# Pools per k tile at a seam, an interleaved last tile pair, a partial sum through DRAM and earlier conditioning products in a hybrid SSD trunk

## The chip, the cores and the metric

The kernel runs on one NeuronCore of a Trainium2 chip. The metric is the device time of one execution in microseconds; a lower one is better. Five engines work side by side, each from its own queue in order: TensorE (PE) with its weight loads (PEld), VectorE (DVE), ScalarE (ACT), GpSimd (POOL) and SyncE (SP). DMA transfers are issued from the queues of SP, ACT and POOL, and sixteen DMA engines carry them.

## The reference

One residual layer over a sequence of 1024 positions with 1024 channels. What matters here:

```python
u = rms_norm(x, ln1) * (1 + scale1) + shift1        # scale, shift, gate: silu(c) @ w_ada + b_ada
gl, cb, cc, cx, z, xbc, dt = split(u @ w_in)        # 2048, 3 x 1024, 2048, 4096, 32 columns
p_conv = (cb * causal_conv3(cc * cx)) @ w_conv_out
xbc = silu(causal_conv4(xbc) + b); xs, bs, cs = split(xbc)
y = ssd_scan(xs * dt, -exp(a_log) * dt, bs, cs) + d_skip * xs     # 8 groups, 32 heads, state 128
y = group_rms_norm(y * silu(z)) * ssm_norm_w
p_ssm = y @ w_ssm_out                                # 2048 -> 1024
x = x + gate1 * ((sigmoid(gl_c) * p_conv + sigmoid(gl_s) * p_ssm) @ w_o)
x = x + gate2 * (square(relu(u2 @ w_up)) @ w_down)   # u2 from x as u, then a final rms_norm
```

The conditioning vectors (six times 1024 numbers) come from a matrix-vector product with w_ada.

## The kernel before

Everything is held transposed: channels on the 128 partitions, the 1024 positions along the free dimension in two halves of 512 columns (H). A float32 product is made of three matmuls in a rounded format: each operand is split into a high part (a cast, on ACT) and a low part (source minus high, on DVE), and high x high, high x low and low x high are added in PSUM. `proj` (L125) does this for one output tile: eight k tiles, two halves, 48 matmuls; `load_w` (L90) loads and splits a weight tile, and `load_w_acc` (L99) gets the low part by an accumulating DMA from POOL instead. `strassen_pair` (L145) makes two output tiles with seven products of half the size, 84 matmuls in place of 96, and needs more sums on DVE. It is used for the last eight gate tiles, for z and for the short convolution; its operands T1 to T4 ("tops") are sums of u's quarters.

The kernel runs through these stages, in the order of the program:

1. norm and modulation of x into the operands uh and ul (L245 to L520), with the first eight gate tiles (gl) as they become ready. uh and ul are 32 tiles of 2 KB per partition, all in one pool `u` on the right side of SBUF;
2. the tops (L526 to L540), in place in the memory of x, four pools xk0 to xk3 of 8 KB, which are then released. On the same memory follows the small pool `p0d` for the dt projection (L541 to L563), and after it `pe1`, the working pool of the Strassen pairs: s12 and s34 of 4 KB, two each of cu, cq, cy of 2 KB, and one buffer wv of 4.1 KB;
3. Strassen pairs for the remaining gates (f = 8 to 14), for z (eight pairs, one per group) and for the short convolution (twelve pairs). The 32 remaining conditioning products (`gemvs`, L569) lie in this stage, four ahead of each of two gate pairs and three ahead of each z pair: each loads a 512 KB row block of w_ada into wv from POOL's queue, and a DVE pass (L319) multiplies it by c and sums it up into a column of mcol. The buffer wv is single, so a load waits for the product before it;
4. for each of eight groups, four xbc tiles (`proj_group` L719, `xbc_tile` L706: projection, copy of both halves into a padded row raw, two activations from PSUM into cacc, three taps on DVE, silu), and beside the next group's tiles the SSD scan of this one (`ssd_group` L731, chunks of 128 positions);
5. the seam (L844): u is released, and on its memory a ring of eight buffers ys of 8 KB (`yy`) is laid. First they hold the eight split tiles of the short convolution's output (loaded through three buffers ccs), the operands of w_conv_out, beside the last group's scan (L860);
6. the SSD projection in four quarters b of four k tiles each (L874 to L930), every quarter eight output tiles f of 24 matmuls. b = 0 writes its partial result to DRAM (s_d). At b = 1 the memory of the scan is released, slots are laid there (`sl`), the stored sums are loaded into them and added to; b = 2 adds and gates, b = 3 adds and splits the merged result. The scale of groups 4 to 7 (`finish` L806, `rstd` L822), which b = 2 needs, is made within b = 0;
7. w_o, then the MLP with Strassen products, and the final norm.

The order of the instructions in each queue is not that of the program: a planner (`schedule_with_timeline_sim=True`) writes it ahead of time from its own model of durations, taking the earlier instruction of the program first among those that it holds to be ready. Pools with `reuse_waits="tile"` let a tile on released memory start once the memory under that tile is free.

Of the kernel before, what the change touches and what calls it, by code (L numbers as in the profile page):

```python
# [8 lines left out]
F32 = mybir.dt.float32  # L9
F32R = mybir.dt.float32r  # L10
# [6 lines left out]
P = 128  # L17
T = 1024
# [20 lines left out]
def hybrid_trunk(tc, xT, par, hrows, crow, wada1, wadak, wada2, win, wdt, wco, wso, wo, wup, wdt_, wdn, out):  # L39
# [3 lines left out]
    def tt(o, a, b, op, eng=dve):  # L43
        return eng.tensor_tensor(out=o, in0=a, in1=b, op=op)  # L44
# [80 lines left out]
    def proj(w, xh, xl, nk=KT, base=0, halves=(0, 1), width=H):  # L125
        wh, wl = w
        ps = [mm.tile([P, H], F32, name="mm")[:, :width] for _ in halves]
        for k in range(nk):
            c0 = base + k * P
            mm3(ps, wh[:, c0:c0 + P], wl[:, c0:c0 + P], [xh[k][h] for h in halves], [xl[k][h] for h in halves],  # L130
                k == 0, k == nk - 1)
        return ps
# [118 lines left out]
    hb = d0.tile([P, 64], F32, name="hb")[:, 0:32]  # L251
    z2 = d0.tile([P, NC_ * NH], F32, name="z2")

    up = tc.alloc_tile_pool(name="u", bufs=1, side="right")
    uh = [[up.tile([P, H], F32R, name=f"uh{k}{h}") for h in (0, 1)] for k in range(KT)]
    ul = [[up.tile([P, H], F32R, name=f"ul{k}{h}") for h in (0, 1)] for k in range(KT)]

    cbp = tc.alloc_tile_pool(name="cbp", bufs=1)
    glp = tc.alloc_tile_pool(name="glp", bufs=2)
# [58 lines left out]
    def gemv(w_, o):  # L318
        return dve.tensor_tensor_reduce(out=w_, in0=w_, in1=cb, scale=0.5, scalar=prm[:, BADA + o:BADA + o + 1],  # L319
                                        op0=ALU.mult, op1=ALU.add, accum_out=mcol[:, o:o + 1])  # L320
# [208 lines left out]
    for k in range(4):  # L529
        tks.append(tc.alloc_tile_pool(name=f"tk{k}", bufs=1, side="right", reuse_waits="tile"))  # L530
        with tc.issue_after(rdy.ins):
            ts4 = tops_of(xt[k] + xt[k + 4], mcol[:, 4 + k:5 + k], dc1[:, k:k + 1])
        for i, t in enumerate(ts4):
            o = [tks[-1].tile([P, H], F32R, name=f"t{i}{j}") for j in (0, 1)]
            split(*o, t)
            X[f"T{i + 1}"].append(o)
        X["11"].append([uh[k][0], ul[k][0]])
        X["21"].append([uh[k + 4][0], ul[k + 4][0]])
        X["22"].append([uh[k + 4][1], ul[k + 4][1]])
        xk[k].release()  # L540
    p0d = tc.alloc_tile_pool(name="p0d", bufs=1, reuse_waits="tile")  # L541
    wdr = p0d.tile([P, KT, NH], F32, name="wdr")
    sp.dma_start(wdr, wdt)
    wd = p0d.tile([P, KT, 2 * NH], F32R, name="wd")
# [15 lines left out]

    act.copy(z2, ps[:, :C2])

    p0d.release()  # L563
    ps0.release()

    pe1 = tc.alloc_tile_pool(name="pe1", bufs=2, reuse_waits="tile")
    gem = iter(range(32))

    def gemvs(n):  # L569
        for _, i in zip(range(n), gem):  # L570
            w_ = pe1.tile([P, T + 32], F32, name="wv", bufs=1)[:, 0:T]
            pool.dma_start(w_, wada2[i])  # L572
            gemv(w_, 16 + i)

    def as3(a):
        return a.rearrange("p (c h) -> p c h", c=NC_)

# [25 lines left out]
    for f in range(8, 16, 2):  # L603
        ts_ = [glp.tile([P, T], F32, name="glt") for _ in (0, 1)]

        def gl_ev(i, h, src):
            act.activation(ts_[i][:, hs[h]], src, AF.Tanh, scale=0.5)

        if f == 10:
            dt_chain()  # L610
        elif f > 10:
            gemvs(4)
        strassen_pair(pe1, win[f], win[f + 1], X, gl_ev)
        for i in (0, 1):
            act.dma_start(gl_d[f + i], ts_[i])
    for g in range(NG):
        ts_ = [glp.tile([P, T], F32, name="glt") for _ in (0, 1)]

        def z_ev(i, h, src):
            t = ts_[i][:, hs[h]]  # L620
            act.activation(t, src, AF.Tanh, scale=0.5)
            stt(t, t, 1.0, src, ALU.add, ALU.mult)

        gemvs(3)
        strassen_pair(pe1, win[gtile(g) + 4], win[gtile(g) + 5], X, z_ev)
        for i in (0, 1):
            act.dma_start(z_d[2 * g + i], ts_[i])
# [70 lines left out]
    psB = tc.alloc_tile_pool(name="psB", bufs=1, space=PSUM)  # L698
    psC = tc.alloc_tile_pool(name="psC", bufs=1, space=PSUM)

    padded = [p2t.tile([P, T + 3], F32, name=f"raw{i}", bufs=1) for i in (0, 1)]
    for raw in padded:
        pool.memset(raw[:, 0:3], 0.0)
    padded = itertools.cycle(padded)

    def xbc_tile(win_i, ci, dst):  # L706
        ps = proj(load_w_acc(win[win_i]), uh, ul)
        raw = next(padded)
        for h in (0, 1):
            act.copy(raw[:, 3 + H * h:3 + H * h + H], ps[h])  # L710
        a = p2t.tile([P, T], F32, name="cacc")
        for h in (0, 1):
            act.activation(a[:, hs[h]], ps[h], AF.Identity, bias=hb[:, ci:ci + 1], scale=hw[:, 4 * ci + 3:4 * ci + 4])  # L713
        for j in (2, 1, 0):
            stt(a, raw[:, j:j + T], hw[:, 4 * ci + j:4 * ci + j + 1], a, ALU.mult, ALU.add)
        act.activation(dst, a, AF.Tanh)
        stt(dst, dst, 1.0, a, ALU.add, ALU.mult)

    def proj_group(g):  # L719
        pg = p2g[g % 2]  # L720
        xs = pg.tile([P, 2, T], F32, name="xs")
        bf = pg.tile([P, T], F32, name="bf")
        cf = pg.tile([P, T], F32, name="cf")
        b = gtile(g)
        xbc_tile(b + 0, 2 * g, xs[:, 0, :])
        xbc_tile(b + 1, 2 * g + 1, xs[:, 1, :])
        xbc_tile(b + 2, 16 + g, bf)
        xbc_tile(b + 3, 24 + g, cf)
        return xs, bf, cf

    def ssd_group(g, xs, bf, cf, prev):  # L731
# [106 lines left out]
    for g in range(NG - 1):  # L838
# [2 lines left out]
        while prev is None:  # L841
            prev = drive(gen)
        cur = proj_group(g + 1)
    up.release()  # L844

    yy = tc.alloc_tile_pool(name="yy", bufs=8, side="right", reuse_waits="tile")
    yc = []
    for f in range(8):
        ccs = pcf.tile([P, T], F32, name="ccs", bufs=3)
        sp.dma_start(ccs, yc_d[f])  # L850
        y = yy.tile([P, 2, T], F32R, name="ys")
        split(y[:, 0, :], y[:, 1, :], ccs)
        yc.append(y)
    ych, ycl = [[[y[:, i, hs[h]] for h in (0, 1)] for y in yc] for i in (0, 1)]
# [19 lines left out]
    for b in range(4):  # L874
        yh, yl = [], []
        for k in range(4):
            kk = 4 * b + k
            if k % 2 == 0:
                rb_ = p4.tile([P, T], F32, name="rb", bufs=1)
                sp.dma_start(rb_, rst_d[kk // 2].partition_broadcast(P))  # L880
            yr = p4.tile([P, T], F32, name="yr")
            sp.dma_start(yr, y_d[kk])
            stt(yr, yr, prm[:, SNW + kk:SNW + kk + 1], rb_, ALU.mult, ALU.mult)
            ys = yy.tile([P, 2, T], F32R, name="ys")
            split(ys[:, 0, :], ys[:, 1, :], yr)
            yh.append([ys[:, 0, hs[0]], ys[:, 0, hs[1]]])
            yl.append([ys[:, 1, hs[0]], ys[:, 1, hs[1]]])
        if b == 1:
            for p_ in (psC, psB, psA, p2, p2g[1], p2g[0]):
                p_.release()  # L890
            sl = tc.alloc_tile_pool(name="slots", bufs=17, reuse_waits="tile")
            p5 = tc.alloc_tile_pool(name="p5", bufs=2, side="right", reuse_waits="tile")
        for f in range(8):
            if f % 2 == 0:
                w = load_w(wso[b, f // 2])
            if b == 0:
                if f == 2:
                    finish(prev, last_mm[0])
                if f == 5:
                    rstd(1)  # L900
                gt = gp.tile([P, T], F32, name="gt")
                ps = proj(w, yh, yl, nk=4, base=(f % 2) * 512)
                for h in (0, 1):
                    act.copy(gt[:, hs[h]], ps[h])
                act.dma_start(s_d[f], gt)
                continue
            if b > 1:
                gt = gp.tile([P, T], F32, name="gt")
                sp.dma_start(gt, gl_d[8 + f])
            if b == 2:  # L910
                pc = p5.tile([P, T], F32, name="pc")
                sp.dma_start(pc, at_d[f])
            ps = proj(w, yh, yl, nk=4, base=(f % 2) * 512)
            for h in (0, 1):
                if b == 1:
                    at[f][h] = sl.tile([P, H], F32, name=f"s{h}")
                    sp.dma_start(at[f][h], s_d[f, :, hs[h]])
                a = at[f][h]
                if b < 3:
                    tt(a, ps[h], a, ALU.add)  # L920
                if b == 2:
                    stt(a, gt[:, hs[h]], 1.0, a, ALU.add, ALU.mult)
                    tt(a, a, pc[:, hs[h]], ALU.add)
                if b == 3:
                    g_ = gt[:, hs[h]]
                    stt(g_, g_, 1.0, ps[h], ALU.add, ALU.mult)
                    tt(a, a, g_, ALU.add)
                    mh[f][h] = sl.tile([P, H], F32R, name=f"s{h}")
                    ml[f][h] = sl.tile([P, H], F32R, name=f"s{h}")
                    split(mh[f][h], ml[f][h], a)  # L930
    p5.release()
    p4.release()
    gp.release()
    yy.release()
    d0.release()

    xp = tc.alloc_tile_pool(name="x1", bufs=1, side="right", reuse_waits="tile")
# [280 lines left out]
```

## Time and profile before

| | us |
|---|---|
| three runs | 2106.05, 2103.34, 2099.37 |
| their median | 2103.34 |
| the profiled execution | 2105.2 |
| its span, first to last instruction | 2103.4 |
| PE busy in the span | 2072.5 |
| DVE busy | 1473.1 |
| ACT busy | 963.0 |
| POOL busy | 182.6 |
| mean granted clock of PE | 0.992 |

A timeline row gives the start, the duration, the engine and line, the operation, what it writes and reads, and in square brackets how long the engine stood idle before it and what ended that. A row of the waits gives the total in us, the number of times and the longest. A row of the stretches gives the length, then the busy time of PE, weight load, DVE, ACT and POOL with their instructions, then the clock, the DMA engines' busy share and GB/s. Line numbers of helpers (L44 subtract or add, L47 scalar-tensor-tensor, L87 and L94 weight load and cast, L109 split's cast, L154 Strassen matmul, L120 to L123 the matmuls of `proj`, L319 a conditioning product) stand for many callers; the tile's name tells which.

### The profile page before, as it was taken

The numbers are of one execution on the slowest core, as the hardware profiler recorded it, in microseconds if no ns is written. First come the engines' busy times: TensorE is split into PE (matmuls) and PEld (weight loads), VectorE is DVE, ScalarE is ACT, GpSimd is POOL, SyncE is SP. The second block draws the span as 40 slices with busy tenths as digits, with TensorE's granted clock in tenths as the row PEclk, the third lists the DMA queues.
The fourth block names the chain that finished last, engine by engine and source line by source line (L and its number), as shares of the span: only waits on it lengthen the run. The fifth ranks groups of instructions, "written<-read, shape, count | busy, mean of one in ns | idle before, by whom it ended". The sixth has DMA issues, their size and how long they took to land.

```text
span 2103.4 us, 26276 instructions
## 1 busy us (share of the span) xinstructions
PE 2072.5 (99%) x9760; PEld 1698.4 (81%) x9760; DVE 1473.1 (70%) x2310; ACT 963.0 (46%) x1600; POOL 182.6 (9%) x251
## 2 busy tenths in 40 slices
PE   8999999999999999999999999999999999999997
PEld 6878877888888888887878788888888888888887
DVE  8757777776637778877796748745866665658775
ACT  4433232332246768676564531224554454544432
POOL 0000000000000000000000000012000001232213
PEclk8999999999999999999999999999999999999998
DMA  8315645222274555555366676453144347988932
GB/s 327 106 64 187 203 161 194 87 70 74 77 202 111 123 123 136 140 142 137 99 207 219 213 282 198 167 194 118 61 165 165 150 157 268 304 239 254 284 75 81
DMA packets 139666, 345.16 MB, mean 164 GB/s; under 512 B 13153, under 2 KB 48353, under 8 KB 138002
## 3 DMA queue, kind: packets, MB, share of 16 engines
q1 hardware_dynamic: 98258, 200.14, 29.8%
q0 software_dynamic: 27856, 107.49, 18.0%
q10 hardware_dynamic: 13424, 35.85, 4.4%
q8 instruction: 77, 1.26, 0.2%
q14 instruction: 51, 0.42, 0.1%
HBM read 270.88 MB, written 72.55 MB: 163 GB/s over the span
## 4 chain that ended last, share of the span: by engine, by line
PE 87%; issue 8%; DMA 2%; DVE 1%; POOL 1%; ACT 0%; SPq 0%; DVEq 0%; POOLq 0%; ACTq 0%
PE mm L154 25%; PE mm L121 13%; PE mm L123 13%; PE mm L120 13%; PE mm L1111 11%; PE B L761 2%; PE mm L398 2%; PE B L766 2%; PE C L783 1%; PE sx L398 1%; PE st L398 1%; DMA wraw<-in_win 1%; POOL wv L572 1%; PE A L738 1%; DMA x<-in_xT 1%
## 5 line engine op out<-in xcount | busy, mean ns | idle before, releaser
L154 PE MATMUL mm<-t,whi 128*128 128x512 f32 x1104 | 340.9, 391 | 4.6 <-DVE cq L44 4.6
L154 PEld LDWEIGHTS mm<-t,whi 128*128 128x128 f32 x1104 | 207.6, 188 | 49.7 <-DVE cq L44 6.7
L154 PE MATMUL mm<-t,wlo 128*128 128x512 f32 x552 | 214.9, 390 | 0.0
L1111 PE MATMUL mm<-op,whi 128*128 128x512 f32 x672 | 207.0, 389 | 0.0
L121 PE MATMUL mm<-ul,whi 128*128 128x512 f32 x512 | 203.7, 398 | 0.0
L120 PE MATMUL mm<-uh,whi 128*128 128x512 f32 x512 | 203.3, 397 | 0.0
L44 DVE TENSOR_TENSOR wlo<-s,whi 128x1024 fp32r<-128x1024 f32 (+1 forms) x124 | 124.0, 1012 | 63.5 <-ACT whi L159 62.6
L123 PE MATMUL mm<-uh,wlo 128*128 128x512 f32 x512 | 162.3, 395 | 0.0
L44 DVE TENSOR_TENSOR wlo<-wraw,whi 128x1024 fp32r<-128x1024 f32 (+1 forms) x132 | 141.1, 1069 | 22.8 <-ACT whi L94 16.1
L120 PE MATMUL mm<-ys,whi 128*128 128x512 f32 x384 | 148.5, 394 | 3.7 <-ACT ys L109 3.7
L121 PE MATMUL mm<-ys,whi 128*128 128x512 f32 x384 | 148.8, 394 | 0.6 <-DVE ys L44 0.6
L47 DVE SCALAR_TENSOR_TENSOR cacc<-raw,hw,cacc 128x1024 f32<-128x1024 f32 x96 | 122.8, 1279 | 37.7 <-ACT cacc L713 37.0
L1111 PEld LDWEIGHTS mm<-op,whi 128*128 128x128 f32 x672 | 126.1, 188 | 26.2
L154 PE MATMUL mm<-s,whi 128*128 128x512 f32 x448 | 138.0, 389 | 0.7 <-ACT cu L177 0.7
L159 ACT CAST whi<-wraw 128x1024 fp32r<-128x1024 f32 x76 | 63.5, 836 | 157.8 <-PE mm L154 128.5
L1111 PE MATMUL mm<-op,wlo 128*128 128x512 f32 x336 | 130.7, 389 | 0.0
L755 ACT ACTIVATE seg<-acb,acum 128x128 f32<-128x128 f32 x256 | 81.9, 395 | 106.6 <-PE B L761 101.5
L47 DVE SCALAR_TENSOR_TENSOR y<-mm,mcol,y 128x512 f32<-128x512 f32 (+1 forms) x100 | 69.3, 704 | 78.1 <-PE mm L1111 41.3
L94 ACT CAST whi<-wraw 128x1024 fp32r<-128x1024 f32 x52 | 54.6, 1052 | 149.2 <-PE mm L121 127.0
L123 PE MATMUL mm<-ys,wlo 128*128 128x512 f32 x384 | 122.6, 394 | 0.0
L159 ACT CAST whi<-s 128x1024 fp32r<-128x1024 f32 x76 | 79.7, 1050 | 91.4 <-PE mm L154 85.3
L154 PEld LDWEIGHTS mm<-t,wlo 128*128 128x128 f32 x552 | 103.9, 188 | 21.7
(309 smaller groups left out, 4575.0 us busy)
## 6 DMA issues: line engine op xcount, KB each, us to landing
wraw<-in_win SPq DMA_DIRECT2D x83, 512.0 KB
dr<-in_wdt_ SPq DMA_DIRECT2D x108, 256.0 KB
op_d<-hp POOLq DMA_DIRECT2D x12, 1792.0 KB, 6.4
hr<-op_d POOLq DMA_DIRECT2D x42, 512.0 KB, 5.9
wv<-in_wada POOLq DMA_DIRECT2D x32, 512.0 KB, 3.8
wlo<-in_win POOLq DMA_DIRECT2D x32, 512.0 KB, 7.1
acb<-ac_d SPq DMA_DIRECT2D x64, 256.0 KB
wraw<-in_wup SPq DMA_DIRECT2D x32, 512.0 KB
```

The costliest lines, as they stand in the source:

```text
L44: return eng.tensor_tensor(out=o, in0=a, in1=b, op=op)
L47: return dve.scalar_tensor_tensor(out=o, in0=a, scalar=s, in1=b, op0=op0, op1=op1)
L94: act.copy(hi, raw)
L120: pe.matmul(o, lhsT=wh, rhs=h_, start=start, stop=False)
L121: pe.matmul(o, lhsT=wh, rhs=l_, start=False, stop=False)
L123: last_mm[0] = pe.matmul(o, lhsT=wl, rhs=h_, start=False, stop=stop)
L154: last_mm[0] = pe.matmul(o, lhsT=l_[:, s_], rhs=r_, start=first and k == j == 0, stop=k == 3 and j == 2, skip_group_check=True)
L159: act.copy(hi, src)
L398: pe.matmul(sps[f, h], lhsT=w_[f][:, j * P:j * P + P], rhs=v_[j][h], start=j == i == 0, stop=j == KT - 1 and i == 2, skip_group_check=True)
L755: act.activation(seg[:, r, :], acb[:, r, :], AF.Relu, bias=acum[:, c, hd:hd + 1], scale=-1.0)
L761: pe.matmul(Bk[o:o + 64, P * (r // 2):P * (r // 2) + P], lhsT=xd[:, r, :], rhs=seg[:, r, :], start=True, stop=True, skip_group_check=True)
L1111: pe.matmul(o, lhsT=l_[:, c_], rhs=t[:, r_, k, :], start=first and k == j == 0, stop=k == 3 and j == 2, skip_group_check=True)
```

## The change

Four edits, in the order of the program.

- Ten of the 32 conditioning products move up to just behind the tops, ahead of the dt projection, into a pool `p0g` with three buffers wv, which lies behind `p0d` on the released memory of x. Two gate pairs then take three each instead of four, the eight z pairs two instead of three.
- The pool u becomes eight pools, one per k tile (uh and ul of both halves, 8 KB), and the ring of ys eight pools of one buffer, so that each ys lies on one k tile of u. They are released and taken in turn.
- An xbc tile's first tap is one activation of 1024 columns from raw in SBUF, not two of 512 from PSUM. raw is padded to T + 32 columns. In the last group the last two xbc tiles are made together, in an order that ends with k tiles 4 to 7 of the second.
- In the SSD projection b = 1 also goes through DRAM: it loads b = 0's sum into gt, adds its own and stores it again. The slots, the release of the scan's memory and the load of the sums move to b = 2, `finish` to b = 1, f = 0 and `rstd(1)` to b = 1, f = 3.

```diff
-    up = tc.alloc_tile_pool(name="u", bufs=1, side="right")
-    uh = [[up.tile([P, H], F32R, name=f"uh{k}{h}") for h in (0, 1)] for k in range(KT)]
-    ul = [[up.tile([P, H], F32R, name=f"ul{k}{h}") for h in (0, 1)] for k in range(KT)]
+    ups_, uh, ul = [], [], []
+    for k in range(KT):
+        up = tc.alloc_tile_pool(name=f"u{k}", bufs=1, side="right")
+        ups_.append(up)
+        for n, u_ in (("uh", uh), ("ul", ul)):
+            u_.append([up.tile([P, H], F32R, name=f"{n}{k}{h}") for h in (0, 1)])
...
+    gem = iter(range(32))
+
+    def gemvs(n, pl, bufs=1):
+        for _, i in zip(range(n), gem):
+            w_ = pl.tile([P, T + 32], F32, name="wv", bufs=bufs)[:, 0:T]
+            pool.dma_start(w_, wada2[i])
+            gemv(w_, 16 + i)
+
     p0d = tc.alloc_tile_pool(name="p0d", bufs=1, reuse_waits="tile")
+    p0g = tc.alloc_tile_pool(name="p0g", bufs=1, reuse_waits="tile")
+    gemvs(10, p0g, 3)
     wdr = p0d.tile([P, KT, NH], F32, name="wdr")
     sp.dma_start(wdr, wdt)
...
         elif f > 10:
-            gemvs(4)
+            gemvs(3, pe1)
...
-        gemvs(3)
+        gemvs(2, pe1)
         strassen_pair(pe1, win[gtile(g) + 4], win[gtile(g) + 5], X, z_ev)
...
-    padded = [p2t.tile([P, T + 3], F32, name=f"raw{i}", bufs=1) for i in (0, 1)]
+    padded = [p2t.tile([P, T + 32], F32, name=f"raw{i}", bufs=1) for i in (0, 1)]
...
     def xbc_tile(win_i, ci, dst):
-        ps = proj(load_w_acc(win[win_i]), uh, ul)
+        xbc_evac(proj(load_w_acc(win[win_i]), uh, ul), ci, dst)
+
+    def xbc_evac(ps, ci, dst):
         raw = next(padded)
         for h in (0, 1):
             act.copy(raw[:, 3 + H * h:3 + H * h + H], ps[h])
         a = p2t.tile([P, T], F32, name="cacc")
-        for h in (0, 1):
-            act.activation(a[:, hs[h]], ps[h], AF.Identity, bias=hb[:, ci:ci + 1], scale=hw[:, 4 * ci + 3:4 * ci + 4])
+        act.activation(a, raw[:, 3:3 + T], AF.Identity, bias=hb[:, ci:ci + 1], scale=hw[:, 4 * ci + 3:4 * ci + 4])
...
-        xbc_tile(b + 2, 16 + g, bf)
-        xbc_tile(b + 3, 24 + g, cf)
+        if g < NG - 1:
+            xbc_tile(b + 2, 16 + g, bf)
+            xbc_tile(b + 3, 24 + g, cf)
+            return xs, bf, cf
+        ws = [load_w_acc(win[b + i]) for i in (2, 3)]
+        ps = [[mm.tile([P, H], F32, name="mm") for _ in hs] for _ in ws]
+        for i, k in [(0, k) for k in range(4)] + [(i, k + 4 - 4 * i) for k in range(4) for i in (0, 1)] + [(1, k) for k in range(4, KT)]:
+            c_ = slice(k * P, k * P + P)
+            mm3(ps[i], ws[i][0][:, c_], ws[i][1][:, c_], uh[k], ul[k], k == 0, k == KT - 1)
+            if (i, k) == (0, KT - 1):
+                xbc_evac(ps[0], 16 + g, bf)
+        xbc_evac(ps[1], 24 + g, cf)
...
-    up.release()
-
-    yy = tc.alloc_tile_pool(name="yy", bufs=8, side="right", reuse_waits="tile")
+    for p_ in reversed(ups_):
+        p_.release()
+
+    yys = [tc.alloc_tile_pool(name=f"yy{f}", bufs=1, side="right", reuse_waits="tile") for f in range(8)]
+    yring = itertools.cycle(yys)
...
-        y = yy.tile([P, 2, T], F32R, name="ys")
+        y = next(yring).tile([P, 2, T], F32R, name="ys")
...
-        if b == 1:
+        if b == 2:
             for p_ in (psC, psB, psA, p2, p2g[1], p2g[0]):
                 p_.release()
             sl = tc.alloc_tile_pool(name="slots", bufs=17, reuse_waits="tile")
...
-            if b == 0:
-                if f == 2:
+            if b < 2:
+                if (b, f) == (1, 0):
                     finish(prev, last_mm[0])
-                if f == 5:
+                if (b, f) == (1, 3):
                     rstd(1)
                 gt = gp.tile([P, T], F32, name="gt")
+                if b == 1:
+                    sp.dma_start(gt, s_d[f])
                 ps = proj(w, yh, yl, nk=4, base=(f % 2) * 512)
                 for h in (0, 1):
-                    act.copy(gt[:, hs[h]], ps[h])
+                    if b == 0:
+                        act.copy(gt[:, hs[h]], ps[h])
+                    else:
+                        tt(gt[:, hs[h]], ps[h], gt[:, hs[h]], ALU.add)
                 act.dma_start(s_d[f], gt)
                 continue
...
-                if b == 1:
+                if b == 2:
                     at[f][h] = sl.tile([P, H], F32, name=f"s{h}")
                     sp.dma_start(at[f][h], s_d[f, :, hs[h]])
```

More of the change, by code (lines that the diff above doesn't have):

```diff
@@ L561, in hybrid_trunk @@
     act.copy(z2, ps[:, :C2])
+    p0g.release()
     p0d.release()
@@ L566, in hybrid_trunk @@
     pe1 = tc.alloc_tile_pool(name="pe1", bufs=2, reuse_waits="tile")
[L567 to L573, printed above, removed]
     def as3(a):
@@ L883, in hybrid_trunk @@
             stt(yr, yr, prm[:, SNW + kk:SNW + kk + 1], rb_, ALU.mult, ALU.mult)
-            ys = yy.tile([P, 2, T], F32R, name="ys")
+            ys = next(yring).tile([P, 2, T], F32R, name="ys")
             split(ys[:, 0, :], ys[:, 1, :], yr)
@@ L933, in hybrid_trunk @@
     gp.release()
-    yy.release()
+    for p_ in reversed(yys):
+        p_.release()
     d0.release()
```

## The prediction

> **What bounds the kernel now.** I read the first page's table, then the view of who waited for whom, then the chain of waits, then timelines of the places that the diff touches.
>
> ```profile
> PE 2072.5 (99%) x9760; PEld 1698.4 (81%) x9760; DVE 1473.1 (70%) x2310; ACT 963.0 (46%) x1600; POOL 182.6 (9%) x251
> ...
> 366.12 231.05 PE mm L154 x1018
> ...
> PE mm L154 <- DVE cq L44: 4.6, 4, 2.6
> PE st L243 <- DVE sdg L44: 4.0, 1, 4.0
> PE mm L120 <- ACT ys L109: 3.7, 1, 3.7
> PE mm L154 <- ACT cu L177: 1.6, 2, 0.9
> PE mm L121 <- DVE ys L44: 0.6, 1, 0.6
> ```
>
> TensorE (PE) is busy for 2072.5 of 2103.4 us, so 30.9 us is all that any edit which keeps the matmuls could win. The chain's long piece gives the pace: 231.05 us for 1018 matmuls, 0.227 us each. In the waits (us in total, times, longest), only three lines lie where the diff works: 4.6 us for the DVE operation cq (Strassen pairs of the first stage), 3.7 + 0.6 us for the split operands ys (the seam), and part of the 1.6 us for cu. The 4.0 us for sdg are the kernel's last microseconds and untouched. The change removes no matmul, so its best case is about 4.6 + 4.3 + 0.9 = 9.8 us, 0.47%; everything else in it can only cost.
>
> **The seam.**
>
> ```profile
> 1060.69 0.48 PE L123 MATMUL mm<-uh,wlo 128*128 128x512 f32 x1
> ...
> 1066.10 1.22 PE L120 MATMUL mm<-ys,whi 128*128 128x512 f32 x2 [3.70 <-ACT ys L109]
> 1067.96 1.22 PE L121 MATMUL mm<-ys,whi 128*128 128x512 f32 x2 [0.63 <-DVE ys L44]
> ...
> 1063.21 1.43 ACT L713 ACTIVATE cacc<-mm,hb,hw 128x512 f32<-128x512 f32 x2
> 1064.53 0.57 ACT L710 COPY raw<-mm 128x512 f32<-128x512 f32 x1
> 1065.00 2.94 ACT L109 CAST ys<-ccs 128x1024 fp32r<-128x1024 f32 x3
> ...
> 1030.00:1061.00 31.00, 31.00 (x169) 24.52 (x168) 21.93 (x42) 17.70 (x38) 1.12 (x2) 1.00 0.39 120
> 1061.00:1092.00 31.00, 26.67 (x124) 21.00 (x124) 30.56 (x44) 22.87 (x41) 0.00 (x0) 0.89 0.55 167
> ```
>
> The first rows are a timeline (start, duration), the last two are stretches (length, then busy time of PE, weight load, DVE, ACT, POOL, then clock, DMA share, GB/s). The last read of u ends at 1061.17. All eight ys buffers lie on u's memory; the first casts come at 1065.00, behind three ACT instructions that serve the last xbc tile, and PE stands 3.70 and then 0.63 us. With a pool per k tile, ys number k needs only u's tile k. In the new order of the last two xbc tiles there are 16 blocks of 6 matmuls, 1.36 us each at 0.227; tile 0 is last read by block 6, tiles 1, 2 and 3 by blocks 8, 10 and 12, tiles 4 to 7 by the last four. So u's tile 0 is free ten blocks = 13.6 us before the last matmul, the next three 10.9, 8.2 and 5.4 us before it. A split costs 0.98 us of ACT (2.94 / 3) and 1.2 of DVE. In the 31 us before the seam DVE is free for 31 - 21.93 = 9.07 us and ACT for 13.3; about half of that falls in the last 13.6 us, room for three splits, and three is also what the ccs ring has preloaded. PE then eats one ys per 1.36 us, or per 2.7 us once the second output tile joins. The first projection tile needs two banks: the first xbc tile of the pair ends five blocks, 6.8 us, before the last, and its banks are free after two copies of 0.57. I take the whole wait: **-4.3 us** (bounds 0 and -4.3). What is late next is DVE: in the 31 us after the seam it was busy for 30.56, and 52.5 us of its work must now fit 57.7 us. A ys that DVE brings late would give back part, priced below as a rival.
>
> **One activation from raw in place of two from PSUM** (32 tiles).
>
> ```profile
> L713 ACT ACTIVATE cacc<-mm,hb,hw x64: 762/785/807, 611.4 to 1072.3; 128x512 f32<-128x512 f32 x64
> L716 ACT ACTIVATE xs<-cacc x16: 1038/1054/1062, 617.4 to 1058.7; 128x1024 f32<-128x1024 f32 x16
> ```
>
> ACT gives 2 x 0.785 for one 128x1024 from SBUF, nearest row 1.05: 0.5 us less per tile, and the bank is free 1.6 us sooner. ACT was busy for 46%, and no PE wait names cacc or raw, so **0**; without that cover it would be a gain.
>
> **Ten products moved up.** Each is a 512 KB load issued by POOL and one DVE pass. The rows: the product's instructions, the planned gap on DVE, and one late product.
>
> ```profile
> L572 POOL DMA_DIRECT2D wv<-in_wada x32: 531/531/557, 166.7 to 365.8; - x32
> L319 DVE CUSTOM_DVE_ANT_0 wv<-wv,cb,prm x32: 1273/1284/1289, 170.8 to 369.6; 128x1024 f32<-128x1024 f32 x32
> DMA to landing us min/median/max: 3.6/3.8/6.3
> ...
> 101.19 7.31 DVE L44 TENSOR_TENSOR t<-x,t 128x512 fp32r<-128x512 f32 x12 [3.44 <-ACT t L109]
> 134.21 1.29 DVE L44 TENSOR_TENSOR s<-wraw 128x512 f32<-128x512 f32 x2 [21.93 <-PE st L558]
> 134.42 0.59 ACT L177 COPY cu<-mm 128x512 f32<-128x512 f32 x1
> 109.00:134.00 25.00, 25.00 (x117) 18.64 (x115) 1.16 (x3) 3.25 (x6) 0.00 (x0) 1.00 0.12 44
> ...
> 284.49 1.28 DVE L319 CUSTOM_DVE_ANT_0 wv<-wv,cb,prm 128x1024 f32<-128x1024 f32 x1 [3.20 <-DMA wv<-in_wada]
> 285.70 0.69 DVE L44 TENSOR_TENSOR cq<-mm,cq 128x512 f32<-128x512 f32 x1
> ```
>
> *Where they leave.* 32 issues from 166.7 to 365.8 are one per 6.42 us: with one buffer, each load waits for the product before it. A pair is 84 matmuls, 19.1 us, and three products are 19.3: the ring, not PE, sets that loop's pace by a hair. At 284.49 DVE stood 3.20 us for such a load, the cq behind it came late, and PE waited for it. With two per pair 12.8 of 19.1 us are needed. Bounds: -4.6 (all of the cq waits) and 0 (the planner may run products ahead, so that their pace stays until they are used up). I take **-3.6**, one wait of about a microsecond staying.
>
> *Where they land.* DVE works 1.16 of the 25 us from 109, DMA is at 0.12; ten products are 10 x (1.28 + 0.08) = 13.6 us. They cannot start before the tops are split (108.5), since their three buffers lie on x. The code's sizes put the first buffer behind 7.3 KB of the small pool, so that it also lies under the first pair's s34 and cu; the tenth product uses that buffer (fourth turn), and ACT's cu copy at 134.42 and PE behind it wait for it. A turn is 0.53 + 3.8 + 1.37 = 5.7 us: the fourth ends at 108.5 + 22.8 = 131.3, in time. With every landing at 6.3, the slowest seen, a turn is 8.2 and the end 141.3, 6.9 us late. As DMA is at 0.12 there, I take 3.8: **0**, bounds 0 and +6.9. The wd split that PE needs at 121.6 stands behind one or two products at most. POOL has no other issue in that time; SP's loads wait for none of these buffers, dt's scratch lies behind them.
>
> **Second quarter through DRAM.** The b = 1 tiles load the stored sum into gt, add, store again; b = 2 reads it into the slots. Eight 512 KB stores and eight 512 KB loads are new; the old slot loads move one quarter later, and the sums over group 7 (finish, rstd) move from b = 0 to b = 1. DVE and PE do the same work as before, and PE had no wait in these quarters, so nothing is won here.
>
> ```profile
> 1225.23 14.22 SPq L917 DMA_DIRECT2D s<-s_d  x14
> ...
> 1221.00:1243.00 22.00, 22.00 (x99) 18.19 (x98) 6.80 (x16) 5.12 (x8) 0.00 (x0) 1.00 0.79 264
> 1243.00:1265.00 22.00, 22.00 (x99) 18.22 (x98) 16.66 (x18) 6.33 (x6) 0.00 (x0) 1.00 0.79 292
> 1265.00:1287.00 22.00, 22.00 (x99) 18.22 (x98) 17.91 (x20) 6.33 (x6) 0.00 (x0) 1.00 0.50 163
> 1287.00:1309.00 22.00, 22.00 (x99) 18.22 (x98) 18.36 (x29) 2.11 (x2) 0.00 (x0) 1.00 0.77 249
> 1309.00:1331.00 22.00, 22.00 (x99) 18.22 (x98) 17.13 (x26) 3.34 (x4) 0.00 (x0) 1.00 0.59 200
> 1240.00:1250.00 10.00, 10.00 (x46) 8.29 (x45) 5.85 (x7) 2.77 (x3) 0.00 (x0) 1.00 1.03 384
> ...
> 1215.33 0.24 ACTq L820 DMA_DIRECT2D ssq_d<-row  x1
> 1220.80 0.24 ACTq L820 DMA_DIRECT2D ssq_d<-row  x1
> 1239.50 0.43 SPq L880 DMA_DIRECT2D rb<-rst_d  x1
> 1262.02 2.35 DVE L44 TENSOR_TENSOR ys<-yr,ys 128x1024 fp32r<-128x1024 f32 x2
> 1277.13 1.29 DVE L44 TENSOR_TENSOR s<-mm,s 128x512 f32<-128x512 f32 x2 [0.18 <-PE mm L123]
> ```
>
> From 1243 to 1331 the DMA engines are full for (0.79 + 0.50 + 0.77 + 0.59) x 22 = 58.3 of 88 us and move 19.9 MB, 341 GB/s when full. The slot loads were issued from 1225 on, mostly before that stretch; in it now come up to 24 transfers, 12.6 MB, 37 us: 95 of 88. Three gt loads fit before it, leaving 91. So the room is gone for a moment: bounds 0 (loads ahead of need, two output tiles of PSUM as a cushion) and +7. The other danger is rstd. The last add of b = 1 at 1277.13 follows its last matmul, and a quarter is 8 x 24 matmuls = 43.6 us, so b = 0 ends at 1233.5. Behind its last matmul now come the two row sums, 5.5 us apart by the two ssq_d stores: the second at 1239.0. Before, 18.7 us passed from that store to the rb load and 24.9 more to the end of the quarter's last split: 1282.6, against 1281.2, where b = 2 needs its fourth k block (1277.1 + 3 x 1.36). That is nearly even, and readiness rather than order may bring it sooner, so I charge **+1.0** for both dangers. On SP, each gt load now waits for a buffer whose store has landed; behind it in that queue stand weights and yr, which PE needs a pair of tiles (10.9 us) and a quarter later.
>
> The Trainium skill ("DMA: Bandwidth & Descriptors", section "Where 436 GB/s comes from") says that for transfers between HBM and SBUF the HBM share of a core, about 358 GB/s, binds, against 435 for the fabric. The stretch from 1240 reads 384 GB/s, above it, so the row disagrees. With the three early gt loads out, 19.9 + 12.6 - 1.6 = 30.9 MB fall into the 88 us: by 358 that would take 86 us, so any late step would show; by 435 it takes 71 and hides.
>
> **Sum**, on the profiled execution (2105.2 us, span 2103.4): -4.3 - 3.6 + 1.0 = -6.9, to 2098.3. The runs' median, 2103.34, lies 1.9 below that execution, so the forecast is **2096.4**.
>
> **Rivals.** (a) *DMA has no room in the second and third quarters*: for it 91 of 88 us; against it, 1240 to 1250 ran full with PE at 10.00 of 10. Costs 7 in place of 1: 2102.4. (b) *DVE takes over the seam*: 30.56 of 31 us speak for it; half the wait, 2.2 us, returns: 2098.6. (c) *The products keep their pace*: 22 at 6.42 us still run to about 308, so most cq waits stay and only about 1 us goes: 2099.0; against it, they are now two per pair. (d) *Slower*: the ten loads do not overlap on POOL's queue and land one per 3.8 us. The first product ends at 108.5 + 0.5 + 3.8 + 1.4 = 114.2, the tenth at 148.4, 14 us after cu's 134.42; PE waits that long, 2096.4 + 14 = 2110.4. It decides from 2.24 us per product (20.2 / 9) on, and outweighs the gains from 3.0. Against it: each engine of the 16 is 0.12 busy there.
>
> **Chances.** Forecast 0.52 (own range 2092 to 2100; 0.42 of it under 2097.0), (a) 0.13, (b) 0.09, (c) 0.08, (d) 0.10, unnamed 0.08. A change of 0.3%, 6.3 us, is about what three runs between 2099 and 2106 tell from none; faster means under 2097.0, slower above 2109.7. Faster 0.42 + 0.02 unnamed; same 0.10 + 0.13 + 0.09 + 0.08 + 0.01; slower 0.10 + 0.05. The range from 2090 to 2107 leaves (d), the slow unnamed and a little below.
>
> **What would show it.** Seam: no ys line among PE's waits, ys casts before the last matmul on uh. Products: ten L319 passes between 112 and 134, cu at about 134.4, and cq waits near 1 us or none. Third quarter: PE still 22.00 of 22; a line of PE waiting for ps or ys near 1277 or a DVE wait for s_d's loads means (a). I am wrong if PE's waits at these places sum to over 7 us, or if PE stands somewhere that has no line above.

## The result, and the profile after

The changed kernel takes **2120.2 us** (median of 2119.7 to 2125.1) where the kernel before, run beside it, takes 2102.3: a ratio of 1.0090, 95% interval 1.0067 to 1.0112. It is slower by some 18 us; the forecast was 2096.4 us with a range of 2090 to 2107. The profiled execution after took 2119.9 us (span 2118.1), 14.7 us more than that of before.

First the top of the page after, then who TensorE waited for between 1030 and 1330 us (us in total, times, longest), and one line of the same view for the whole span.

```profile
PE 2076.0 (98%) x9760; PEld 1700.6 (80%) x9760; DVE 1472.6 (70%) x2310; ACT 961.0 (45%) x1568; POOL 182.0 (9%) x251
...
PE mm L120 <- ACT ys L109: 13.0, 2, 8.8
PE mm L120 <- DVE s L44: 2.2, 1, 2.2
PE mm L120 <- ACT gt L926: 0.9, 1, 0.9
...
PE mm L154 <- DVE cq L44: 0.6, 1, 0.6
```

As many matmuls and nearly the same busy time on TensorE, but new waits: 13.0 us for ys. They are not at the seam. The seam in TensorE's timeline after (start, duration), and the stretch that ends there (length, then busy time of PE, weight load, DVE, ACT and POOL, then clock, DMA share, GB/s):

```profile
1043.41 0.61 PE L123 MATMUL mm<-uh,wlo 128*128 128x512 f32 x2
1043.86 0.39 PE L120 MATMUL mm<-ys,whi 128*128 128x512 f32 x1
...
1013.00:1044.00 31.00, 31.00 (x159) 25.58 (x158) 30.89 (x46) 22.37 (x38) 0.00 (x0) 1.00 0.40 118
```

The seam is gone as forecast: the last matmul on u is followed by the first on ys without a gap. The time is lost 220 us later, where b = 2 of the SSD projection begins:

```profile
1265.93 0.61 PE L123 MATMUL mm<-ys,wlo 128*128 128x512 f32 x2
1275.39 2.08 PE L120 MATMUL mm<-ys,whi 128*128 128x512 f32 x4 [8.84 <-ACT ys L109]
...
1288.03 2.08 PE L120 MATMUL mm<-ys,whi 128*128 128x512 f32 x4 [4.20 <-ACT ys L109]
...
1297.50 0.50 PE L120 MATMUL mm<-ys,whi 128*128 128x512 f32 x1 [2.15 <-DVE s L44]
```

Behind each of these three waits the matmuls themselves are slow. The stretches from there on after, and then the stretch behind the seam's wait before (columns as above; the last but two is the granted clock, the last but one the DMA engines' busy share):

```profile
1275.40:1278.00 2.60, 2.60 (x6) 2.12 (x7) 2.39 (x3) 1.05 (x1) 0.00 (x0) 0.50 1.05 404
1278.00:1281.40 3.40, 3.40 (x9) 2.59 (x9) 0.00 (x0) 0.00 (x0) 0.00 (x0) 0.53 1.06 393
...
1283.40:1288.00 4.60, 0.44 (x2) 0.01 (x1) 1.28 (x1) 1.04 (x1) 0.00 (x0) 1.00 1.03 403
1288.00:1291.00 3.00, 2.97 (x7) 2.40 (x8) 2.42 (x2) 0.53 (x1) 0.00 (x0) 0.51 1.03 369
...
1297.50:1301.70 4.20, 4.20 (x11) 3.31 (x12) 4.20 (x6) 1.48 (x2) 0.00 (x0) 0.59 0.05 19
```

```profile
1066.00:1069.00 3.00, 2.26 (x5) 1.35 (x6) 3.00 (x5) 3.00 (x6) 0.00 (x0) 0.50 0.82 216
```

Each of these waits is followed by some microseconds at about half the clock (0.50 to 0.59 in these rows): about 0.43 us a matmul in place of 0.227. Adding up what each matmul took over 0.227 in those places gives 6.2 us after (31 matmuls behind three waits) and about 2.4 us before (12 matmuls behind the seam).

So the books of the two profiled executions are: the first Strassen stage ends 6.9 us earlier (at 590.3 in place of 597.2); of the seam 4.3 + 2.4 = 6.7 us are gone; waits of 8.84 + 4.20 + 2.15 + 0.94 = 16.1 us are new, with 6.2 of slow matmuls; and the part behind the SSD projection is 3.5 us longer, with two waits of TensorE for y in the down projection, of 1.20 and 1.71 us, that end at 1927 and 2006. Together that is +12.2 of the 14.7; the other 2.5 lie scattered in the stretch of the scan, and I assign them to nothing.

**Why ys is late at b = 2.** One chain, followed backwards. SyncE's queue, VectorE and ScalarE after:

```profile
1267.34 0.38 SPq L899 DMA_DIRECT2D rb<-rst_d  x1
1267.77 9.20 SPq L941 DMA_DIRECT2D s<-s_d  x11
1277.07 0.38 SPq L899 DMA_DIRECT2D rb<-rst_d  x1
...
1272.97 2.48 DVE L47 SCALAR_TENSOR_TENSOR yr<-yr,prm,rb 128x1024 f32<-128x1024 f32 x2 [4.19 <-DMA rb<-rst_d]
1285.62 1.28 DVE L47 SCALAR_TENSOR_TENSOR yr<-yr,prm,rb 128x1024 f32<-128x1024 f32 x1 [7.82 <-DMA yr<-y_d]
...
1274.29 1.04 ACT L109 CAST ys<-yr 128x1024 fp32r<-128x1024 f32 x1 [7.11 <-DMA s_d<-gt]
```

ys waits for yr, yr for rb, rb for the rsqrt of the sums over group 7, and these for the scan. The end of that scan and of its sums, from the groups of zs and ssq_d, before and then after (count: duration, first and last start):

```profile
L44 DVE TENSOR_TENSOR zs<-xs,zs x16: 1214/1216/1219, 724.4 to 1199.7; 128x1024 f32<-128x1024 f32 x16
L820 ACTq DMA_DIRECT2D ssq_d<-row x16: 221/224/460, 764.1 to 1220.8; - x16
L738 PE MATMUL A<-cf,bf x104: 270/273/377, 657.1 to 1060.3; 128*128 128x128 f32 x104
```

```profile
L44 DVE TENSOR_TENSOR zs<-xs,zs x16: 1218/1222/1229, 718.4 to 1231.8; 128x1024 f32<-128x1024 f32 x16
L837 ACTq DMA_DIRECT2D ssq_d<-row x16: 221/227/454, 758.1 to 1252.9; - x16
L755 PE MATMUL A<-cf,bf x94: 270/273/377, 650.9 to 1035.9; 128*128 128x128 f32 x94
```

The scan of group 7 ends **32 us later** after, although TensorE has finished with u 17 us earlier. The third row of each says how: it counts the products of cf and bf that stand ahead of the last matmul on u, two per chunk of the scan. Before, 52 of the 64 chunks stood there; after, 47. Something in the change made the planner put the projections first and the scan behind.

### The profile page after: what moved, and what is told of

It is laid out like the page before. It is cut to its first block, busy times and chain, and to the rows that moved or that the text cites. A ratio compares the mean times of both kernels' runs of the same rounds, so it can differ in the third digit from the quotient of the medians.

```text
span 2118.1 us, 26262 instructions
## 1 busy us (share of the span) xinstructions
PE 2076.0 (98%) x9760; PEld 1700.6 (80%) x9760; DVE 1472.6 (70%) x2310; ACT 961.0 (45%) x1568; POOL 182.0 (9%) x251
## 4 chain that ended last, share of the span: by engine, by line
PE 86%; issue 6%; DMA 4%; DVE 3%; ACT 0%; POOL 0%; SPq 0%; DVEq 0%; POOLq 0%; ACTq 0%
PE mm L154 28%; PE mm L120 13%; PE mm L123 13%; PE mm L121 13%; PE mm L1136 9%; PE B L778 2%; PE mm L401 2%; PE B L783 2%; PE C L800 1%; DMA dr<-in_wdt_ 1%; PE st L401 1%; PE sx L401 1%; PE A L755 1%; DMA wv<-in_wada 1%; DMA y_d<-zs 1%
## 5 line engine op out<-in xcount | busy, mean ns | idle before, releaser
L120 PE MATMUL mm<-ys,whi 128*128 128x512 f32 x384 | 151.5, 402 | 16.1 <-ACT ys L109 13.0
L121 PE MATMUL mm<-ys,whi 128*128 128x512 f32 x384 | 151.8, 399 | 0.0
L123 PE MATMUL mm<-ys,wlo 128*128 128x512 f32 x384 | 129.0, 397 | 0.0
```

Of the source, the lines that this page charges most:

```text
L120: pe.matmul(o, lhsT=wh, rhs=h_, start=start, stop=False)
L121: pe.matmul(o, lhsT=wh, rhs=l_, start=False, stop=False)
L123: last_mm[0] = pe.matmul(o, lhsT=wl, rhs=h_, start=False, stop=stop)
```

## The experiments

Two theories at the start. **Theory 1**: the second quarter through DRAM is the culprit, by its traffic or by the row sums that now stand behind b = 0. **Theory 2**: the one activation from raw is, because with it the planner writes another order; the trip through DRAM only stands at the place where the late scan is felt. Moving the calls of finish and rstd has no run of its own; the run with the second quarter alone holds it too.

All ratios below are to the kernel before, run on the same chip beside it.

### The second quarter as before

Of the edit, the two conditions that matter; finish and rstd go back into b = 0 with it.

```diff
-        if b == 2:
+        if b == 1:
...
-            if b < 2:
+            if b == 0:
...
```

> The changed kernel with the second quarter of the SSD projection as before (slots taken and loaded in b = 1, sums of group 7 at the end of b = 0); the seam, the one activation and the ten products stay. Theory 1 (the trip through DRAM is the culprit, by its traffic or by the later row sums): everything it lost goes away, no PE wait from 1180 to 1300, about 2091 to 2094. Theory 2 (the one activation makes the planner put the scan later; the trip through DRAM only passes the delay on): the scan still ends near 1230; the slots lie on the scan's memory, so PE must now wait in b = 1 for the scan, the row sums and the slot loads. In the written order the last row sum stands behind the 624th matmul on ys, 48 into b = 1, which is all that PSUM holds. A wait of 15 to 30 us there, 2110 to 2125.

2123.2 us, 1.0082 (1.0067 to 1.0097): nothing of the loss comes back. TensorE's waits:

```profile
PE mm L120 <- DVE s L44: 9.2, 2, 7.7
PE C L834 <- ACT sqh L109: 7.1, 1, 7.1
```

Theory 1 falls; theory 2 had the place and the time. The loss has only moved: the slots lie on the scan's memory, so b = 1 now waits for the scan, the row sums (7.1 us) and the slots' loads (7.7).

### The second quarter alone

The same edit the other way round, in the kernel before.

> The kernel before with nothing but the second quarter through DRAM. Theory 1 (the traffic or the later row sums are enough by themselves): PE waits of 10 us or more near the start of b = 2 and 2112 to 2120. Theory 2 (only with a late scan): the scan ends as before near 1198 and the sums at about 1239, nearly even with the need as forecast; PE waits near 1277 of 0 to 3 us, 2102 to 2106. The forecast's rival of full DMA engines would be a wait for ps or s_d of about 7 us, 2109.

2105.8 us, 1.0003 (0.9993 to 1.0012). The only line that TensorE's waits have between 1200 and 1330 us, and the end of the sums:

```profile
PE mm L120 <- DVE gt L44: 0.3, 1, 0.3
...
L820 ACTq DMA_DIRECT2D ssq_d<-row x16: 221/222/460, 759.0 to 1235.6; - x16
```

Eight stores and eight loads of 512 KB more cost nothing that can be measured. The first matmul of b = 2 starts at 1271.6 there, 36 us after the last ssq_d store; after, that store at 1252.9 came 13.6 us before the end of the last matmul of b = 1 (1266.5), too late.

### The one activation alone

raw is padded to T + 32 columns with it.

```diff
-        for h in (0, 1):
-            act.activation(a[:, hs[h]], ps[h], AF.Identity, ...)
+        act.activation(a, raw[:, 3:3 + T], AF.Identity, ...)
```

> The kernel before with one edit: the first tap of an xbc tile is one activation from raw in place of two from PSUM. The forecast charged it 0. Theory 1 (the trip through DRAM is the culprit): 2102, no difference. Theory 2 (this edit alone sets the scan back): in the written order 48 of the 64 chunks stand ahead of the last matmul on u where the kernel before has 52, and the last row sum 108 matmuls (24 us) later; PE then waits in b = 1 for the slots, 10 to 25 us with its slow matmuls behind: 2110 to 2125.

2115.5 us, 1.0047 (1.0030 to 1.0064): the edit that the forecast charged with nothing costs about 10 us by itself.

```profile
PE mm L120 <- DVE s L44: 11.3, 3, 9.3
PE mm L120 <- ACT ys L109: 0.5, 1, 0.5
...
L737 PE MATMUL A<-cf,bf x96: 270/274/377, 657.6 to 1051.9; 128*128 128x128 f32 x96
```

48 chunks ahead of the seam, a wait of 9.3 us in b = 1 for slots, and, second row, hardly a wait for ys at the seam, with u still in one pool.

### The two activations put back

The same edit undone in the changed kernel.

> The changed kernel with the two activations from PSUM put back; pools per k tile, the pair of xbc tiles, the ten products and the trip through DRAM stay. Theory 1: as slow as after, 2115 to 2122, with the waits at the start of b = 2. Theory 2: 51 chunks stand ahead of the last matmul on u, group 7's zs comes near 1190, the sums are ready about when b = 2 needs them; seam and first stage keep their gains (6.9 and at least 4.3): 2090 to 2096, faster than both kernels.

2106.7 us, 1.0008 (0.9995 to 1.0020). Half a hit: the waits at b = 2 are gone, as theory 2 said, but there is no gain over the kernel before. TensorE's timeline at the seam:

```profile
1057.71 0.71 PE L784 MATMUL B<-cf,state 128*128 128x128 f32 x4
1063.86 1.19 PE L801 MATMUL C<-xe,bt 128*128 128x256 f32 x2 [5.44 <-DVE xe L44]
```

The wait for ys has turned into one for xe, a step of the scan that VectorE makes late because it is busy: from 1057.2 to 1063.3 it works without a gap, on a weight split, a split of ys, two operations of 1.2 us on xs and the scan's small steps. That is the forecast's rival (b) in kind, with a wait of 5.4 us where it had 2.2.

### The ten products alone

> The kernel before with nothing but the ten conditioning products moved up. The forecast gave -3.6 (bounds 0 and -4.6, and up to +6.9 where they land). The profiled executions so far had the end of the first Strassen stage 6.9, 4.0 and 5.5 us earlier with the ten products moved, but also 5.2 and 0.1 us earlier without. Theory A (a steady gain): 3 to 6 us less than before. Theory B (the waits for cq vary between executions, and the execution of before was a bad one): 0 to 2 us less, with PE's waits for cq near 1 us.

2104.9 us, 0.9999 (0.9989 to 1.0009): no gain that can be measured; at most 2.3 us. The time is that of theory B, but its reason, that the execution of before was a bad one, is not borne out (below). The profiled execution is the slowest of the twelve, at 2109.2 us. In it cq cost TensorE 2.2 us and cu 3.7:

```profile
PE mm L154 <- ACT cu L177: 3.7, 2, 3.1
PE mm L154 <- DVE cq L44: 2.2, 3, 1.3
```

The cq wait of 4.6 us in the execution of before was not an odd one. In the five profiled executions without this edit cq cost 4.6, 0.7, 4.1, 4.5 and 3.6 us, in the nine with it between 0.6 and 2.6: 3.5 and 1.9 on average. Some of the cq waits do go, then, about 1.6 us. Against that stands cu: 1.6 us in each of the five, between 1.6 and 3.7 in the nine. In the execution here the tenth product starts at 135.2, and ACT's copy of cu waits 2.01 us for it, until 136.50; that is the mechanism of the forecast's rival (d), in small.

### Pools and pair alone

The last two xbc tiles together and the pools per k tile, with two activations, in the kernel before.

> The kernel before with the pools per k tile and the pair of xbc tiles alone; activations, products and the second quarter as before. If the seam's gain comes from the pools: the ys wait of 3.7 us and the slow matmuls behind it go, 2 to 8 us less than before. If it came from the one activation (fewer chunks of the scan ahead of the seam, so less VectorE work there): a wait of the scan for VectorE of 4 to 6 us takes its place, as in the run with the two activations put back, and the time is that of before within 2 us.

2107.8 us, 1.0015 (1.0003 to 1.0026). Second alternative by its wait, the same 5.4 us for xe as above, at the seam; the time lies 3.1 us above the kernel before, a little more than the 2 that were expected. The pools do let ys start early; what they free is taken by VectorE.

### Two activations that read raw

```diff
-            act.activation(a[:, hs[h]], ps[h], AF.Identity, ...)
+            act.activation(a[:, hs[h]], raw[:, 3 + H * h:3 + H * h + H], AF.Identity, ...)
```

> The kernel before with the first tap as two activations of 512 columns that read raw in SBUF: the banks come free as early as with the one activation, but there is no single one. In the written order 50 chunks stand ahead of the last matmul on u (52 before, 48 with one activation alone), and the last row sum behind matmul 572 on ys (516 and 624). If the row sums' place sets the loss: between the two, the sums end at about the start of b = 1, the slots come 5 to 8 us late or just in time, 2103 to 2111, and no wait at the 624th matmul as long as the 9.7 us there with one activation. If the single instruction itself is the cause (its duration, not the order): as before, 2102 to 2106.

2113.7 us, 1.0041 (1.0027 to 1.0055).

```profile
PE mm L120 <- DVE s L44: 2.5, 1, 2.5
PE mm L120 <- DVE gt L47: 4.9, 1, 4.9
```

The place was right, the time lies above the range of 2103 to 2111: the wait for slots is 2.5 us (9.3 with the single activation), but one of 4.9 us at 1089, until gt had emptied a conv tile's banks, was not expected. So the loss does not need the single instruction; reading raw is enough.

### GpSimd takes part of the seam

The two activations and the second quarter are as before here; what is new:

```diff
-        split(y[:, 0, :], y[:, 1, :], ccs)
+        act.copy(y[:, 0, :], ccs)
+        tt(y[:, 1, :], ccs, y[:, 0, :].bitcast(F32), ALU.subtract, eng=pool)
-        ps = proj(load_w(wco[f]), ych, ycl)
+        ps = proj(load_w_acc(wco[f]), ych, ycl)
```

> A try for a faster kernel: pools per k tile, the pair and the ten products; two activations and the second quarter as before; and VectorE relieved in the conv product: GpSimd forms the low half of the eight yc tiles, and the low half of wco's weights is accumulated by DMA. If VectorE is what holds the seam once the pools are split (8 x 1.2 + 8 x 1.2 = 19 us of its work go), PE stands there under 1 us: 2092 to 2099. If GpSimd's own time (about 3 us a tile by its 1.55 us for half of one) or its queue makes ys late: a wait for ys of 3 to 10 us, 2102 to 2110.

2109.1 us, 1.0024 (1.0013 to 1.0034): inside the second range, but not by its mechanism: TensorE waits at the seam for steps of the scan and not for ys. These waits, then GpSimd and VectorE there:

```profile
PE C L801 <- DVE xe L44: 6.4, 1, 6.4
PE B L779 <- DVE xs L47: 2.6, 1, 2.6
...
1058.38 2.74 POOL L44 TENSOR_TENSOR ys<-ccs,ys 128x1024 fp32r<-128x1024 f32 x1
...
1058.82 2.85 DVE L44 TENSOR_TENSOR seg<-seg,smk 128x512 f32<-128x512 f32 x1
```

So the steps of the scan came late there even with VectorE relieved. The trace shows a part of why. Some operations of VectorE that ran while GpSimd formed a low half took far longer than elsewhere in the run: seg 2.85 and 2.87 us in place of 0.68, one xs 2.72 in place of 1.22, one zs 3.43 in place of 1.22, one state 1.91 in place of 0.41. Those with an operand in PSUM kept their time (xd, t and xe 0.42), and of those with both operands in SBUF some did as well. The first wait, for xs, stands right behind the seg shown. No run tells what these stretches cost in time.

### The order pinned

All four edits, with only the order held: projection tile t may start no earlier than the chunk that stood ahead of it in the kernel before. The edit in short, with the lists of chunks as comments:

```diff
+            mk.append(pe.matmul(A[:, 0:P], ...))          # a mark per chunk of the scan
...
+        with tc.issue_after(mk[n[t] - 1].ins):            # n: 0,0,0,0,0,0,4,6,8,8,12, ... 46,48,48
+            ps = proj(w, uh, ul)                          # conv tiles: 52,52,55,56,59,60,62,64
```

> The changed kernel, all four edits in, with one thing added: the first matmul of each projection tile on u, and of each conv tile, is held in TensorE's queue behind as many chunks of the scan as in the kernel before (edges of order only, no new work). In the written order 50 chunks then stand ahead of the last matmul on u (47 after, 52 before), and the last row sum behind matmul 606 on ys (705 after). Theory 2 (the order sets the loss): no wait at the start of b = 2, 2100 to 2106, seam wait back. If the loss is in the instruction or in the second quarter's traffic whatever the order: the waits of 9 and 4 us at b = 2 stay, 2115 to 2122.

2103.6 us, 0.9995 (0.9985 to 1.0005). Between 1030 and 1330 us TensorE waits, and the scan ends:

```profile
PE B L793 <- DVE t L44: 2.8, 1, 2.8
PE C L815 <- DVE xe L44: 1.0, 1, 1.0
...
L44 DVE TENSOR_TENSOR zs<-xs,zs x16: 1215/1220/1223, 719.6 to 1193.3; 128x1024 f32<-128x1024 f32 x16
```

The instructions of the change, 17 us less (2120.2 and 2103.6, from two sets of runs), and no wait is left at b = 2: the order alone makes the loss. This is the run that settles it.

### The order pinned up to the seam only

> As the run with the pinned order, but the conv tiles are not held, so the scan may run later from the seam on: 14 chunks stand behind the seam, the last at matmul 377 on ys, and the row sums at 576 to 606 as with the second quarter through DRAM alone. If the seam's wait is VectorE work of the scan that falls together with the splits, it shrinks to 2 us or less here, and nothing is late at b = 2: 2097 to 2101, faster than before. If the seam is as full as before: 2101 to 2106.

**2098.5 us, 0.9971 (0.9960 to 0.9982): faster than both.** Its waits between 1030 and 1330 us:

```profile
PE B L793 <- DVE t L44: 0.4, 1, 0.4
PE mm L120 <- DVE gt L44: 0.4, 1, 0.4
...
L44 DVE TENSOR_TENSOR zs<-xs,zs x16: 1214/1218/1221, 720.5 to 1201.4; 128x1024 f32<-128x1024 f32 x16
...
1030.00:1061.00 31.00, 31.00 (x164) 24.93 (x163) 25.26 (x47) 22.84 (x45) 0.00 (x0) 1.00 0.55 165
```

The chunks of groups 6 and 7 may slide behind the first conv tiles, so the seam, in the last row, is full at clock 1.00; the scan ends at 1201.4 (two us later than before), and as the second quarter goes through DRAM, the sums are needed only at b = 2, where they are in time. The time is 5.3 us less than before. In the two profiled executions the stretch from the last matmul of the first Strassen stage to the last one on ys takes 761.3 us here (592.7 to 1354.0) and 767.2 before (597.2 to 1364.4), 5.9 less, near the seam's 6.7; the first stage was 4.2 us shorter as well, so which of the two the timed 5.3 us are is not shown. The seam is won here without a loss at b = 2.

### The scan ahead

The same pins with up to three chunks more ahead of each tile.

> Seam, one activation and ten products as in the changed kernel, the second quarter as before, and the projection tiles held behind up to three chunks of the scan more than in the kernel before; 55 chunks stand ahead of the last matmul on u. If the scan can run that fast: less scan work at the seam, 2097 to 2103. If the scan is limited by its own chain of steps: PE waits for VectorE and ScalarE between 700 and 1050, several waits of 1 to 4 us, 2106 to 2125.

2141.1 us, 1.0176 (1.0159 to 1.0193).

```profile
PE A L770 <- DVE cf L47: 25.7, 3, 13.5
```

Second alternative, and worse than its range: TensorE stands before a chunk whose cf is not made yet. The scan cannot be pushed ahead of the projections that feed it.

### The slot loads behind yr

```diff
+    last_yr = sp.dma_start(yr, y_d[kk])
...
+                    with tc.issue_after(last_yr.ins) if f > 1 else contextlib.nullcontext():
                         sp.dma_start(at[f][h], s_d[f, :, hs[h]])
```

> The changed kernel with the slot loads of b = 2 from the third output tile on queued on SyncE behind the last yr load of b = 2; after, 11 of 16 stood ahead of the second rb load. The first wait (9 us, until the first ys of b = 2) is the chain from the row sums and stays by either theory. If the second and third wait (4.35 and 2.3 us and the slow matmuls behind them) come from the burst of slot loads: they go or halve, 2110 to 2116. If they come from the chain too (row sums too late): 2118 to 2122.

2116.6 us, 1.0056 (1.0040 to 1.0072), in the changed kernel's order of the scan.

```profile
PE mm L120 <- ACT ys L109: 11.5, 2, 10.0
```

The first wait stays (10.0 us), the second falls from 4.2 to 1.4, the third goes. So by the trace the larger part of the loss at b = 2 is the late sums, and a smaller one the eleven slot loads that stood ahead of the second rb load. By time the smaller part is not shown: the four runs took 2113.3, 2113.5, 2119.7 and 2119.8 us, the profile is of one of the two lower ones, and the other two are as slow as after. The median lies 12.8 us above its kernel before, where after lies 17.9 above, and the two intervals overlap.

## Why the prediction was wrong

**The step that failed is "one activation from raw in place of two from PSUM: 0".** It asked two questions, how long ScalarE takes and whether a wait of TensorE names cacc or raw, and "without that cover it would be a gain". It did not ask what the planner makes of banks that come free 1.6 us sooner, a number that the step itself worked out. The runs put the edit at +10 us alone, and at +13 in the changed kernel (2120.2 against 2106.7 without it, from two sets of runs). With the order held, the whole change measures 0.9995, so no such cost is left. That early banks are what the planner answered to was argued, not shown: two activations that read raw free them as early and move the order too (50 chunks ahead of the seam), the single one moves it further (48), and why was not separated.

**Second quarter through DRAM, +1.0: right for the scan it assumed.** Alone it measures 0.0003 of the time, and at most 2.5 us. The step worked out that rstd would be "nearly even" from a scan that ends as before. Under the changed order the second ssq_d store comes at 1252.9, not at the 1239.0 that the step used, and the first ys of b = 2 at 1274 to 1275, when b = 2 was due at 1266.5: "nearly even" had no reserve for another term's side effect.

**Seam, -4.3: it happened, for another reason, and was undersized.** Pools and pair alone only turn the wait into one for xe; the seam came free after because the scan's chunks had moved behind it. With the single activation alone, and u in one pool, the wait for ys shrinks to 0.5 us as well. The forecast's rival (b), VectorE takes over the seam, was right about the pools and had 0.09. The price of the seam lacked the 12 matmuls at half clock behind the wait, 2.4 us: the row that showed it, 1.22 us for two matmuls, was quoted and not read.

**Ten products, -3.6: not borne out in time.** Alone the edit gives 0.9999, a gain of 2.3 us at most. The cq waits do shrink, by about 1.6 us between the two groups of executions, where the forecast took 3.6. Where the products land, after ran as forecast, the ten between 113.5 and 134 and cu at 134.12; in the run with the ten products alone the tenth was late and TensorE waited 3.1 us for cu: the 0 there was the middle of something that varies.

**The rivals.** By the forecast's own sign, a line of TensorE waiting for ys near 1277, (a), full DMA engines, would have been the cause. The engines are full after from 1275 to 1291 (1.03 to 1.06) at up to 404 GB/s, and the second wait, of 4.20 us, lies in that stretch; but the first wait was there before it, and the runs with the second quarter alone and with the order pinned carry the same sixteen transfers more and show no such wait. The prediction weighed the Trainium skill, "DMA: Bandwidth & Descriptors", section "Where 436 GB/s comes from", and its bound of about 358 GB/s for transfers from HBM: the stretch at 404 disagrees again. (d), the ten loads late, did not come in after, and only in small in the run with the ten products alone. The slower side was held to be (d), at 0.10, and none of the forecast's mechanisms was the order. The forecast did name the sign of being wrong: waits at these places over 7 us in sum; they sum to 16.1. The 3.5 us behind the SSD projection stay open: waits for y of 0.7 to 2.2 us appear in the down projection in several of the runs, whether the change is in or not.

## What to carry to other kernels

Where a planner writes the order, an edit that looks local to one engine with room to spare can reorder everything behind it (52 chunks ahead of the seam became 48 here); count in the written order, before and after, how far each long chain has come at the next seam. A chain that is "nearly even" at one place has to be repriced with every other edit of the same change in. And if an edit is good but its order is not, edges of order alone can put it right: that was worth some 22 us here (2120.2 to 2098.5, from two sets of runs).

## What the runs showed of the hardware

A wait on TensorE can cost more than its length, but does not always. In one run (the GpSimd try) 1.84 us of waiting was followed by a mean clock of 0.60 over 4 us; in another (pinned up to the seam) 2.59 us at the same place left it at 1.00:

```profile
286.98 0.72 PE L154 MATMUL mm<-t,whi 128*128 128x512 f32 x2 [1.84 <-DVE cq L44]
287.00:291.00 4.00, 4.00 (x11) 3.20 (x12) 3.13 (x4) 2.96 (x4) 0.15 (x1) 0.60 0.40 131
```

```profile
285.43 0.73 PE L154 MATMUL mm<-t,whi 128*128 128x512 f32 x2 [2.59 <-DVE cq L44]
285.20:289.20 4.00, 3.77 (x17) 3.12 (x18) 3.05 (x5) 3.01 (x4) 0.40 (x1) 1.00 0.40 131
```

The Trainium skill, "TensorE: Matmul & The Clock Gate", section "What's actually happening", says that the clock halves after an idle window of about 3.4 us that runs freely and is full again after as long a busy one. Half clock and the varying onset agree with the rows here; the 1.84 and 2.15 us waits that were enough are shorter than a whole window, so by these rows a wait need not fill one. For a forecast on this kernel: by the waits read here, those of about 2 to 5 us on TensorE cost between nothing and 2.4 us more than they show.
